# Lo parts of the attention key weights on VectorE, all hi parts on ScalarE, in a one-core hybrid decoder layer

## The chip, the cores and the metric

The kernel runs on one core of a Trainium2 chip. The metric is the device time of one execution in microseconds. Five engines run their own instruction queues, each in order: PE (matmul, with PEld for its weight loads), DVE (VectorE), ACT (ScalarE), POOL (GpSimd) and SP, which here only issues DMAs.

## The reference

One decoder layer over 2048 positions of width 1024: an RMS norm and one input projection feed three mixers, each multiplied by a SiLU gate, and one output projection adds to the residual.

```python
# A) forgetting attention, 8 heads of 64, q and k RMS-normed, c = cumsum(log_sigmoid(f))
sc = q @ k.T * scale + (c[t] - c[s]);  p = softmax(where(s <= t, sc, NEG));  o = p @ v
# B) causal window means over 2/4/8/16 positions minus the token, a 64x64 map per group
# C) stick-breaking attention, 4 heads of 64, strictly causal
log_1m_beta = where(s < t, -softplus(z), 0);  rest = reverse_cumsum(log_1m_beta) - log_1m_beta
a = where(s < t, exp(log_sigmoid(z) + rest), 0);  o = a @ v
out = x + concat(A * silu(g), B * silu(g), C * silu(g)) @ w_out
```

## The kernel before

Rows stand in reverse order in memory, so a query block i (128 rows, 16 blocks) sees keys j*128 to 2048 with j = 15 - i, that is (i+1)*128 of them. All matmuls are float16 pairs: a number is written as a hi part and a lo part (the rest), and three products (hi-hi, hi-lo, lo-hi) are summed in PSUM.

The work falls into four stages that overlap on PE. Phase a is heads 0 to 3 of the forgetting attention, phase b heads 4 to 7, phase s the stick-breaking heads with the pooling mixer among them, and last the output projection. A phase projects q, k, v and gate of block i while the heads of an earlier block run. By the trace below, the attention of a lies at about 58 to 444 us, that of b at 444 to 803, that of s at 803 to 1250, and what is left of the output projection runs to 1416.

A head of a block has one part of keys, or two (96 parts in 64 heads of a phase, of 128 to 1024 columns). What happens to a part in a and b:

- PE makes the scores in one of two PSUM tiles of the pool `sp` (L404), and DVE adds the forget bias, takes the row maximum and writes the tile `L` to SBUF (L736). Only then can PE reuse that PSUM tile.
- ACT takes the exponential in place (L746). `split_t` then writes the hi part as float16 into `pp` (L430 on ACT or L432 on DVE, by the patterns `FHIA` and `FHIB`), and the lo part beside it (L433, a subtraction, on POOL by `FLO`).
- SP issues one DMA transpose of `pp` into `tt` (L435), and PE multiplies `tt` with the values (L446, L447).

In s, ACT takes a sigmoid of the scores into `rr` (L875), POOL masks the first 128 columns of the first part and sets a start column (L877, L878), DVE runs a product scan along the keys (L883), and `split_t` makes hi (ACT, `SHI`) and lo (POOL, `SLO`) of the scan's result, which is transposed and multiplied as before (L903 to L905).

The parts of the softmax or stick weights are what the change calls key weights. `pairs16` (L339) makes the other pairs: hi on ACT, lo on DVE. Of each block it makes those of q and k (tiles `sta`, `stb`, `sts`), of the values and of x (`ppx`); L467 and L469 copy the transposed keys and queries into place on DVE. POOL also has the gain product of k (L718), the division by the softmax sum (L759), the stick rest (L887, L909), the first gate product (L1034) and 16 small DMA issues (L563).

The order of each engine's queue comes from two places: the Python program (a plan that advances the projections against the heads, with lead times by table), and the tile framework's scheduler, which plays the program through a timeline model while it builds it and lets ready instructions pass others. So a change of engine for one instruction can move others.

Of the kernel before, what the change touches and what calls it, by code (L numbers as in the profile page):

```python
# [18 lines left out]
P = 128  # L19
# [44 lines left out]
DEPTH = 3  # L64
TB = 4
PB = 5
FHIA = 'sv'
FHIB = 'ssv'
FLO = 'gg'
SHI = 's'  # L70
SLO = 'gg'
LX = 3
PAT = [5, 7, 9, 10, 11, 12, 12, 12, 13, 14, 14, 14, 15, 15, 15, 15]
XTRA = 29
# [51 lines left out]
def hybrid(ctx: ExitStack, tc, xN, w_in, w_pT, w_out, ng, b_f, qg, kg, w_pool, p_scale, bands, out):  # L126
    nc = tc.nc
    v, s, g, t, sy = nc.vector, nc.scalar, nc.gpsimd, nc.tensor, nc.sync
    S = xN.shape[0]
# [13 lines left out]
    def first(n):  # L143
        return tc.high_priority(offset=n) if n else nullcontext()

    def pick(pattern, k):
        return {"v": v, "g": g, "s": s}[pattern[k % len(pattern)]]
# [240 lines left out]
    def chunks(base):  # L388

        if S - base <= CH:  # L390
            return [(base, S)]
        cut = (base + (512 if base % 512 == 0 else 0)) // 512 * 512 + 512 if not BAL else (S - 512 if base >= S - 1536 else S - CH)
        cut = S - CH if not BAL else cut
        return [(base, cut), (cut, S)]

    def scores(h, qT, Kc, c0, c1_, tag, mask):
        sp = ps.tile([P, 1024], F32, name=f"sp{tag}", tag="sp")
        off = c0 % 512
        b = c0
        while b < c1_:  # L400
            e = min(c1_, (b // 512 + 1) * 512)
            m_ = mask and b == c0
            for a in range(2):
                t.matmul(sp[:, b - c0 + off:e - c0 + off], qT[:, a * NH + h, :], Kc[b // 512][:, h, b % 512:b % 512 + e - b], start=(a == 0), stop=(a == 1 and not m_))  # L404
            if m_:
                t.matmul(sp[:, off:off + P], id16, cmask, start=False, stop=True)
            b = e
        return sp[:, off:off + c1_ - c0]

    def group(n):  # L410

        return 4 if n <= GR4 * P else 2 if n <= GR2 * P else 1
# [3 lines left out]
    def split_t(p32, n, tag, h, all_, hi_eng, lo_eng):  # L416

        G = group(all_)
        k = h % G
        if k == 0:  # L420
            shared["pp"] = at.tile([P, 2 * CH], F16, name=f"pp{tag}", tag="pp", bufs=PB)
            shared["tt"] = at.tile([P, 2 * CH // P, P], F16, name=f"tt{tag}", tag="tt", bufs=TB)
        if G == 1:
            pp, tt = shared.pop("pp"), shared.pop("tt")
        else:
            pp, tt = shared["pp"], shared["tt"]
        o_ = 2 * n * k
        hi, lo = pp[:, o_:o_ + n], pp[:, o_ + n:o_ + 2 * n]
        if hi_eng is s:
            s.copy(hi, p32)  # L430
        else:
            hi_eng.tensor_copy(hi, p32)  # L432
        lo_eng.tensor_tensor(lo, p32, hi, ALU.subtract)  # L433
        if k == G - 1:
            sy.dma_start_transpose(tt[:, :2 * n * G // P, :], pp[:, :2 * n * G])  # L435
        return tt[:, o_ // P:(o_ + 2 * n) // P]
# [57 lines left out]
    class Fox:  # L494
# [227 lines left out]
        def qk(self, i, h):  # L722
            ph, negc = self.ph, self.negc
            j = NT - 1 - i
            qT = self.ctx[i]
            cs = list(chunks(j * P))
            n_ = len(cs)
            mm = sm.tile([P, 2], F32, name=f"mm{ph}_{i}_{h}", tag="mm")
            ls = []
            for a, (c0, c1_) in enumerate(cs):  # L730
                tag = f"{ph}_{i}_{h}_{a}"
                sp = scores(h, qT, self.Kc, c0, c1_, tag, a == 0)
                lt = at.tile([P, CH], F32, name=f"L{tag}", tag="L", bufs=LB)
                lt = lt[:, :c1_ - c0]
                with first(HSP):
                    v.tensor_tensor_reduce(lt, sp, negc[:, h, c0:c1_], c1[:, 0:1], 4 * NEG if a == 0 else mm[:, a - 1:a],  # L736
                                           ALU.add, ALU.max, mm[:, a:a + 1])
                ls.append(lt)
            nm = sm.tile([P, 1], F32, name=f"nm{ph}_{i}_{h}", tag="nm")
            v.tensor_scalar(nm, mm[:, n_ - 1:n_], -1.0, math.log(PS), ALU.mult, ALU.add)  # L740
            if h == 0:
                self.la = sm.tile([P, 2, NH], F32, name=f"la{ph}_{i}", tag="la")
            la = self.la
            parts = []
            for a, (c0, c1_) in enumerate(cs):
                s.activation(ls[a], ls[a], AF.Exp, bias=nm[:, 0:1], accum_out=la[:, a, h:h + 1])  # L746
                tt = split_t(ls[a], c1_ - c0, f"{ph}_{i}_{h}_{a}", h, S - j * P, pick(FHIA if ph == "a" else FHIB, h + a), pick(FLO, h + a))
                parts.append((c0, c1_, tt))
            return parts, (la, n_)

# [36 lines left out]
    class Stick(Fox):  # L787
# [74 lines left out]
        def qk(self, i, h):  # L862
# [6 lines left out]
            for a, (c0, c1_) in enumerate(chunks(j * P)):  # L869
# [14 lines left out]
                rprev = rr[:, n:n + 1]  # L884
                tt = split_t(rr[:, 0:n], n, tag, h, S - j * P, pick(SHI, h + a), pick(SLO, h + a))
                parts.append((c0, c1_, tt))
# [34 lines left out]
    class Pool:  # L921
        ph = "p"
# [91 lines left out]
    class Out:  # L1014
        ph = "o"
# [200 lines left out]
    with tc.manual_schedule(engines={mybir.EngineType.PE}) if MAN else nullcontext():  # L1216
        opening()
        for k, (n, i) in enumerate(plan):
            ph = phases[n]
# [93 lines left out]
```

## Time and profile before

| | us |
|---|---|
| median of 3 runs (1416.5 to 1421.29) | 1419.98 |
| the profiled execution | 1417.73 |
| its span, first to last instruction | 1415.7 |
| PE busy | 1209.6 (85%) |
| DVE busy | 997.1 (70%) |
| ACT busy | 702.0 (50%) |
| POOL busy | 634.1 (45%) |
| mean granted TensorE clock | 0.937 |

The busy shares are means over stages. PE is the busiest engine and is idle for 206 us of the span. An idle PE is read from the waits: which engine or transfer released the instruction that PE stood before.

### The profile page before, as it was taken

What the parts mean: (1) busy time and instruction counts of PE and PEld (TensorE: products, weight loads), DVE (VectorE), ACT (ScalarE), POOL (GpSimd) and SP (SyncE); (2) the same over time, 40 slices, a digit from 0 to 9 for tenths busy, and PEclk for the clock granted to TensorE, in tenths of its full rate; (3) what the DMA queues carried; (4) which work ended last, traced back from release to release, by engine and by line L of the source; (5) the groups of instructions that cost most, each with busy time, mean ns of one, the idle gap of its engine ahead of it and who ended that gap; (6) DMA issues with size and microseconds to landing.
All of it is one profiled execution on the core that took longest, in us unless ns stands there. A gap on an engine that the chain in (4) does not pass through costs nothing.

```text
span 1415.7 us, 24981 instructions
## 1 busy us (share of the span) xinstructions
PE 1209.6 (85%) x9068; PEld 642.2 (45%) x9068; DVE 997.1 (70%) x2093; ACT 702.0 (50%) x1356; POOL 634.1 (45%) x615
## 2 busy tenths in 40 slices
PE   7788879787887889897987888978988997779998
PEld 3344445444444445454544544444544553444443
DVE  5777889889998567786888655556574669865731
ACT  6555546555554446664667644545455564432210
POOL 0133345445455234553656654555455464623300
PEclk9889899999998989999999999999999999989999
DMA  6689999998999999996999998687886888999853
GB/s 215 176 169 203 214 188 221 200 196 182 210 210 209 210 227 207 202 177 135 184 217 191 227 207 186 146 158 161 173 175 142 172 196 226 225 277 287 225 160 89
DMA packets 617068, 275.25 MB, mean 194 GB/s; under 512 B 552561, under 2 KB 590833, under 8 KB 616945
## 3 DMA queue, kind: packets, MB, share of 16 engines
q1 hardware_dynamic: 605600, 239.93, 80.4%
q10 hardware_dynamic: 10832, 33.67, 7.9%
q8 instruction: 71, 1.16, 0.4%
q14 instruction: 53, 0.43, 0.1%
q0 software_dynamic: 512, 0.07, 0.0%
HBM read 102.60 MB, written 34.67 MB: 97 GB/s over the span
## 4 chain that ended last, share of the span: by engine, by line
PE 18%; DVE 11%; issue 9%; DMA 8%; POOL 8%; ACT 5%; SPq 1%; POOLq 0%; ACTq 0%; DVEq 0%
PE pr L319 11%; DVE rrs L883 5%; POOL pps L433 5%; DMA qTs<-sts 2%; DMA qTb<-stb 2%; PE pqks L319 2%; DVE Lb L736 2%; DMA xTm<-ppm 1%; ACT pps L430 1%; ACT Lb L746 1%; POOL rrs L877 1%; PE sps L404 1%; DMA ttb<-ppb 1%; PE pp L319 1%; POOL ppb L433 1%
## 5 line engine op out<-in xcount | busy, mean ns | idle before, releaser
L433 POOL TENSOR_TENSOR ppb<-Lb,ppb 128x1024 f16<-128x1024 f32 (+7 forms) x96 | 151.6, 1593 | 150.3 <-ACT ppb L430 68.9
L433 POOL TENSOR_TENSOR ppa<-La,ppa 128x1024 f16<-128x1024 f32 (+7 forms) x96 | 152.7, 1604 | 141.9 <-DVE ppa L432 53.4
L433 POOL TENSOR_TENSOR pps<-rrs,pps 128x640 f16<-128x640 f32 (+7 forms) x96 | 171.3, 1790 | 75.2 <-ACT pps L430 74.8
L319 PE MATMUL pr<-wo,xTm 128*128 128x512 f16 x768 | 172.2, 386 | 8.1 <-DMA xTm<-ppm 5.3
L883 DVE TENSOR_TENSOR_SCAN rrs<-rrs 128x640 f32<-128x640 f32 (+7 forms) x64 | 109.5, 1714 | 68.3 <-POOL rrs L877 43.8
L430 ACT CAST pps<-rrs 128x640 f16<-128x640 f32 (+7 forms) x96 | 76.1, 796 | 142.0 <-DVE rrs L883 127.3
L746 ACT ACTIVATE Lb<-Lb,nmb 128x640 f32<-128x640 f32 (+7 forms) x96 | 85.6, 892 | 80.3 <-DVE nmb L740 75.4
L746 ACT ACTIVATE La<-La,nma 128x640 f32<-128x640 f32 (+7 forms) x96 | 85.5, 891 | 77.0 <-DVE nma L740 53.5
L319 PEld LDWEIGHTS <-xTm 128*128 128x128 f16 x768 | 75.8, 99 | 100.9 <-issue 8.8
L319 PEld LDWEIGHTS <-xTb 128*128 128x128 f16 x768 | 77.0, 103 | 92.6 <-issue 16.7
L404 PE MATMUL spa<-Ka,qTa 128*128 128x512 f16 (+3 forms) x320 | 83.7, 371 | 36.8 <-DVE mma L736 35.2
L319 PEld LDWEIGHTS <-xTs 128*128 128x128 f16 x768 | 74.4, 99 | 86.9 <-issue 3.3
L319 PEld LDWEIGHTS <-xTx 128*128 128x128 f16 x720 | 72.6, 105 | 89.3 <-issue 25.5
L319 PE MATMUL pqkb<-wb,xTb 128*128 128x512 f16 x384 | 101.7, 408 | 0.3 <-ACT wb L277 0.3
L404 PE MATMUL spb<-Kb,qTb 128*128 128x512 f16 (+3 forms) x320 | 79.7, 361 | 23.4 <-DVE mmb L736 20.7
L319 PE MATMUL pp<-auxp,xTp 128*128 128x512 f16 x384 | 96.9, 404 | 0.0
L319 PE MATMUL pqka<-wa,xTx 128*128 128x512 f16 x336 | 95.3, 434 | 1.3 <-DVE cr L562 1.3
L319 PE MATMUL pvgb<-wb,xTb 128*128 128x512 f16 x384 | 96.1, 390 | 0.0
L875 ACT ACTIVATE rrs<-sps,nc 128x640 f32<-128x640 f32 (+7 forms) x96 | 80.5, 863 | 30.3 <-PE sps L404 28.8
L319 PE MATMUL pqks<-ws,xTs 128*128 128x512 f16 x384 | 92.1, 385 | 0.7 <-DVE vo L342 0.4
L404 PE MATMUL sps<-Ks,qTs 128*128 128x512 f16 (+3 forms) x320 | 73.2, 361 | 21.2 <-DVE qTs L469 16.6
L319 PE MATMUL pvgs<-ws,xTs 128*128 128x512 f16 x384 | 90.9, 379 | 0.0
(307 smaller groups left out, 2804.4 us busy)
## 6 DMA issues: line engine op xcount, KB each, us to landing
xn<-in_xN_dram SPq DMA_DIRECT2D x16, 512.0 KB, 5.5
xTd<-xTx ACTq DMA_DIRECT2D x16, 512.0 KB, 4.3
xTb<-xTd ACTq DMA_DIRECT2D x16, 512.0 KB, 4.6
xTs<-xTd ACTq DMA_DIRECT2D x16, 512.0 KB, 4.3
xTp<-xTd ACTq DMA_DIRECT2D x16, 512.0 KB, 4.3
go<-gat SPq DMA_DIRECT2D x16, 512.0 KB, 7.6
mt<-mix SPq DMA_DIRECT2D x16, 512.0 KB, 5.6
xr<-in_xN_dram SPq DMA_DIRECT2D x16, 512.0 KB, 4.4
```

Source lines behind the costliest of these rows:

```text
L319: t.matmul(psum, x[:, xa, kt, :], wt[:, wa, c0:c0 + n], start=(kt == 0 and i == 0), stop=(kt == KT - 1 and i == 2))
L404: t.matmul(sp[:, b - c0 + off:e - c0 + off], qT[:, a * NH + h, :], Kc[b // 512][:, h, b % 512:b % 512 + e - b], start=(a == 0), stop=(a == ...
L430: s.copy(hi, p32)
L433: lo_eng.tensor_tensor(lo, p32, hi, ALU.subtract)
L736: v.tensor_tensor_reduce(lt, sp, negc[:, h, c0:c1_], c1[:, 0:1], 4 * NEG if a == 0 else mm[:, a - 1:a], ALU.add, ALU.max, mm[:, a:a + 1])
L746: s.activation(ls[a], ls[a], AF.Exp, bias=nm[:, 0:1], accum_out=la[:, a, h:h + 1])
L875: s.activation(gg, sp, AF.Sigmoid, scale=self.nc2[:, 0:1])
L877: g.affine_select(gg[:, 0:P], gg[:, 0:P], [[1, P]], ALU.is_gt, 1.0, base=0, channel_multiplier=-1)
L883: v.tensor_tensor_scan(gg, gg, gg, init, ALU.mult, ALU.bypass)
```

## The change

Two pattern constants become one, and three patterns change. In a and b the hi part of every part goes to ACT (before: every second in a, two of three in b, the rest on DVE). In a, b and s the lo part of every part goes to DVE (before: POOL). One line less at the top moves every later line number up by one: L433 of before is L432 after.

```diff
-FHIA = 'sv'
-FHIB = 'ssv'
-FLO = 'gg'
+FHI = 's'
+FLO = 'v'
 SHI = 's'
-SLO = 'gg'
+SLO = 'v'
...
                 s.activation(ls[a], ls[a], AF.Exp, bias=nm[:, 0:1], accum_out=la[:, a, h:h + 1])
-                tt = split_t(ls[a], c1_ - c0, f"{ph}_{i}_{h}_{a}", h, S - j * P, pick(FHIA if ph == "a" else FHIB, h + a), pick(FLO, h + a))
+                tt = split_t(ls[a], c1_ - c0, f"{ph}_{i}_{h}_{a}", h, S - j * P, pick(FHI, h + a), pick(FLO, h + a))
```

In the first place, DVE's queue where block 8 of phase a runs its heads 1 and 2, the rows before are these (`La_8_2_0` is the tile of block 8, head 2, part 0; `oma` collects results of the block before, `sta` and `qTa` are queries and keys of the next):

```order
L736 ISA La_8_2_0_2740,mma_8_2_2733<-spa_8_2_0_2734,negca_510,c1_170 128x640
L736 ISA mma_8_2_2733 128x1
L342 SCALAR_TENSOR_TENSOR sta_9_2633<-qna_9_2616,sta_9_2633 128x4x64
L740 TENSOR_SCALAR nma_8_1_2682<-mma_8_1_2668 128x1
L780 TENSOR_REDUCE oma_7_2556<-oa_7_2_2715 128x64
L342 SCALAR_TENSOR_TENSOR sta_9_2633<-qna_9_2616,sta_9_2633 128x4x64
L532 SCALAR_TENSOR_TENSOR u10_2808<-pf10_2791,iwa_300,bft_164 128x8
L736 ISA La_8_2_1_2745,mma_8_2_2733<-spa_8_2_1_2742,negca_510,mma_8_2_2733,c1_170 128x512
L736 ISA mma_8_2_2733 128x1
L533 SCALAR_TENSOR_TENSOR u10_2808<-pf10_2791,iwa_300,u10_2808 128x8
L432 CAST ppa_8_1_0_2685<-La_8_1_0_2675 128x640
```

Of the changed kernel, the rows at the same place on DVE are:

```order
L432 TENSOR_TENSOR ppa_8_0_0_2597<-La_8_0_0_2586,ppa_8_0_0_2597 128x640
L432 TENSOR_TENSOR ppa_8_0_1_2603<-La_8_0_1_2591,ppa_8_0_1_2603 128x512
L341 SCALAR_TENSOR_TENSOR sta_9_2633<-qna_9_2616,sta_9_2633 128x4x64
L735 ISA La_8_2_0_2740,mma_8_2_2733<-spa_8_2_0_2734,negca_510,c1_170 128x640
L735 ISA mma_8_2_2733 128x1
L544 TENSOR_SCALAR u10_2808<-u10_2808 128x8
L341 SCALAR_TENSOR_TENSOR sta_9_2633<-qna_9_2616,sta_9_2633 128x4x64
L735 ISA La_8_2_1_2745,mma_8_2_2733<-spa_8_2_1_2742,negca_510,mma_8_2_2733,c1_170 128x512
L735 ISA mma_8_2_2733 128x1
L432 TENSOR_TENSOR ppa_8_1_0_2685<-La_8_1_0_2675,ppa_8_1_0_2685 128x640
L432 TENSOR_TENSOR ppa_8_1_1_2691<-La_8_1_1_2680,ppa_8_1_1_2691 128x512
```

The two lo parts of head 0 now stand ahead of the bias step of head 2 (the step that frees PE's score tile), and those of head 1 behind it; the cast of head 1 is gone to ACT.

In the second place, POOL's queue in block 11 of phase s, the rows before are these (`pps` is the pair, `rrs` the scan's tile, `left` the rest of the stick):

```order
L887 COPY left_11_12797<-rrs_11_0_1_12818 128x1
L433 TENSOR_TENSOR pps_11_0_0_12810<-rrs_11_0_0_12803,pps_11_0_0_12810 128x1024
L433 TENSOR_TENSOR pps_11_0_1_12822<-rrs_11_0_1_12818,pps_11_0_1_12822 128x512
L878 MEMSET rrs_11_2_0_12968 128x1
L877 AFFINE_SELECT rrs_11_1_0_12887<-rrs_11_1_0_12887 128x128
L887 COPY left_11_12797<-rrs_11_1_1_12902 128x1
L433 TENSOR_TENSOR pps_11_1_0_12894<-rrs_11_1_0_12887,pps_11_1_0_12894 128x1024
L433 TENSOR_TENSOR pps_11_1_1_12906<-rrs_11_1_1_12902,pps_11_1_1_12906 128x512
```

and those of the changed kernel, at the same place on POOL:

```order
L886 COPY left_11_12797<-rrs_11_0_1_12818 128x1
L877 MEMSET rrs_11_2_0_12968 128x1
L876 AFFINE_SELECT rrs_11_1_0_12887<-rrs_11_1_0_12887 128x128
L886 COPY left_11_12797<-rrs_11_1_1_12902 128x1
L877 MEMSET rrs_11_3_0_13072 128x1
L876 AFFINE_SELECT rrs_11_2_0_12968<-rrs_11_2_0_12968 128x128
L886 COPY left_11_12797<-rrs_11_2_1_12983 128x1
```

The mask of head 1 stood behind both lo parts of head 0; now no lo part stands between two masks. `left` of head 0 still stands ahead of it.

In the third place, DVE's queue in the same block of phase s of the changed kernel, the lo parts come in behind the scans that make them (L882 is the scan, L880 the copy of its last column into the second part's start):

```order
L882 SCALAR_TENSOR_TENSOR rrs_11_1_0_12887<-rrs_11_1_0_12887 128x1024
L880 COPY rrs_11_1_1_12902<-rrs_11_1_0_12887 128x1
L882 SCALAR_TENSOR_TENSOR rrs_11_1_1_12902<-rrs_11_1_1_12902,rrs_11_1_0_12887 128x512
L432 TENSOR_TENSOR pps_11_1_0_12894<-rrs_11_1_0_12887,pps_11_1_0_12894 128x1024
L466 COPY Ks_12_12840<-qTs_12_12839 128x4x128
L432 TENSOR_TENSOR pps_11_1_1_12906<-rrs_11_1_1_12902,pps_11_1_1_12906 128x512
L468 COPY qTs_12_12839<-qTs_12_12839 64x512 x2
L882 SCALAR_TENSOR_TENSOR rrs_11_2_0_12968<-rrs_11_2_0_12968 128x1024
```

Before, the next head's scan followed with only L467 and L469 between them; now both lo parts stand there too.

On ACT, one sigmoid of the first stick block moves ahead of the last exponentials of phase b, which adds two loads of ACT's function table (six before, eight after, the first at the kernel's start among them).

## Rows read from the trace of the kernel before

**Rows 1.** The page, part 1: busy us (share of the span) and instructions.
```profile
PE 1209.6 (85%) x9068; PEld 642.2 (45%) x9068; DVE 997.1 (70%) x2093; ACT 702.0 (50%) x1356; POOL 634.1 (45%) x615
```
**Rows 2.** Busy us by stage (a, b, s, output), granted clock, DMA share, GB/s.
```profile
core 0: us, PE busy (x) PEld busy (x) DVE busy (x) ACT busy (x) POOL busy (x), PEclk, DMA share, GB/s
57.90:444.00 386.10, 318.21 (x2422) 172.35 (x2422) 330.41 (x876) 213.18 (x479) 180.93 (x141) 0.90 0.97 198
444.00:803.00 359.00, 308.29 (x2321) 169.55 (x2320) 260.80 (x627) 204.80 (x433) 178.12 (x137) 0.95 0.97 197
803.00:1250.00 447.00, 385.65 (x3320) 207.26 (x3320) 287.87 (x343) 224.29 (x349) 243.15 (x310) 0.94 0.84 185
1250.00:1415.70 165.70, 152.05 (x806) 70.34 (x803) 80.69 (x126) 25.30 (x23) 27.84 (x11) 0.96 0.73 203
```
**Rows 3.** Waits over the whole span: who for whom, us, times, longest.
```profile
ACT pps L430 <- DVE rrs L883: 127.3, 78, 5.7
DVE rrs L883 <- POOL rrs L877: 43.8, 28, 4.1
PE spa L404 <- DVE mma L736: 35.2, 20, 4.9
DVE rrs L883 <- POOL rrs L878: 23.8, 9, 3.9
PE spb L404 <- DVE mmb L736: 20.7, 13, 4.1
PE ob L446 <- DMA ttb<-ppb: 20.6, 16, 3.9
PE pd L821 <- ACT vr L341: 18.5, 5, 7.8
PE sps L404 <- DVE qTs L469: 16.6, 5, 7.1
PE oa L446 <- DMA tta<-ppa: 10.7, 6, 3.2
```
**Rows 4.** Groups on POOL, DVE, ACT: busy us, mean ns, idle before and releaser.
```profile
L433 POOL TENSOR_TENSOR pps<-rrs,pps 128x640 f16<-128x640 f32 (+7 forms) x96 | 171.3, 1790 | 75.2 <-ACT pps L430 74.8 <-issue 0.2
L433 POOL TENSOR_TENSOR ppa<-La,ppa 128x1024 f16<-128x1024 f32 (+7 forms) x96 | 152.7, 1604 | 141.9 <-DVE ppa L432 53.4 <-ACT ppa L430 36.3 <-ACT La L746 7.4
L432 DVE CAST ppa<-La 128x1024 f16<-128x1024 f32 (+7 forms) x48 | 28.4, 592 | 12.5 <-ACT La L746 5.2 <-ACT Va L341 3.8 <-DMA tta<-ppa 3.3
L432 DVE CAST ppb<-Lb 128x1024 f16<-128x1024 f32 (+7 forms) x24 | 13.6, 567 | 8.8 <-ACT Lb L746 8.6
L430 ACT CAST ppa<-La 128x1024 f16<-128x1024 f32 (+7 forms) x48 | 37.6, 784 | 4.2 <-DMA xTx<-ppx 3.8
L875 ACT ACT_TABLE_LOAD x3 | 3.8, 1283 | 0.1
L221 DVE TENSOR_TENSOR q_qka<-fa 128x8 f32<-128x8 f32 x16 | 7.4, 465 | 1.7 <-ACT fa L219 1.7
```
**Rows 5.** Single lines on DVE: xcount, ns min/median/max, first and last start.
```profile
L1036 DVE TENSOR_TENSOR mt<-mt,sg x16: 1214/1226/3369, 1185.2 to 1358.5; 128x1024 f32<-128x1024 f32 x16
L221 DVE TENSOR_TENSOR q_qka<-fa x16: 148/158/2012, 42.1 to 381.1; 128x8 f32<-128x8 f32 x16
L469 DVE COPY qTs<-qTs x32: 285/289/2261, 765.0 to 1179.4; 64x512 f16<-64x512 f16 x32
```
**Rows 6.** Timeline at 199 us: start us, us, engine and instruction.
```profile
199.82 4.21 POOL L433 TENSOR_TENSOR ppa<-La,ppa 128x1024 f16<-128x1024 f32 x2 [1.45 <-DVE rla L757]
199.86 2.11 DVE L758 TENSOR_SCALAR rla<-rla,iva 128x4 f32<-128x4 f32 x1
```
**Rows 7.** Timeline at 1116 us, phase s.
```profile
1115.94 2.13 POOL L433 TENSOR_TENSOR pps<-rrs,pps 128x1024 f16<-128x1024 f32 x1
1118.07 0.29 POOL L877 TENSOR_SCALAR_AFFINE_SELECT rrs<-rrs 128x128 f32<-128x128 f32 x1
1118.39 1.76 DVE L883 TENSOR_TENSOR_SCAN rrs<-rrs 128x768 f32<-128x768 f32 x1 [1.27 <-POOL rrs L877]
```

## The prediction

> **What bounds the kernel now.** I read the page's busy shares first [rows 1]: PE is busy for 1209.6 of 1415.7 us, DVE for 997.1, POOL for 634.1. No other engine comes near PE, so time can only be won from PE's 206 us of idleness, or lost by adding to it. The table by stages [rows 2] shows where it lies: 386.1 - 318.2 = 68 us in a, 51 in b, 61 in s, 14 in the output stage. It shows also that DVE is no average engine in a: 330.4 of 386.1 us, 0.86, against 0.73 in b and 0.64 in s.
>
> Third come the waits [rows 3]. In a and b PE stands before score matmuls until DVE has emptied a PSUM tile (35.2 us and 20.7 us), and before value matmuls until a transpose of a weight pair lands (10.7 and 20.6 us). In s, PE waits for an ACT cast of the values (18.5 us in 5 waits) and for DVE's copies of the queries (16.6 us in 5). Behind these stands a ring: ACT's casts wait for DVE's scans (127.3 us), and the scans wait for POOL's mask and start column (43.8 + 23.8 = 67.6 us). The reader can see one turn of it [rows 7]: a lo subtraction holds POOL until 1118.07, the mask of the next head follows it, and the scan starts at 1118.39 after an idle wait of 1.27 us.
>
> Last, I looked at how long equal instructions take. A DVE instruction on 128x8 elements has a median of 158 ns and a maximum of 2012, a copy of 64x512 a median of 289 and a maximum of 2261 [rows 5]. At 199.82 us one sees why [rows 6]: POOL starts a subtraction, DVE starts a 128x4 instruction 0.04 us later, and it takes 2.11 us. It ended at 201.97, just as the first of the two subtractions in that row was over. So a POOL subtraction can stop DVE for its whole length.
>
> The Trainium skill, "SBUF — State Buffer", Who interferes with whom, says the same as a rule: GpSimd's only SBUF port pair is VectorE's second, locked for a whole instruction. The trace agrees by those 2.11 us.
>
> **The change, part by part.**
>
> *The 72 hi casts that leave DVE.* DVE loses 28.4 us in a and 13.6 in b [rows 4]. ACT gains 48 x 784 ns = 38 us in a and 24 x 784 = 19 in b; it then has 251 of 386 and 224 of 359 us. It waits more than it works there, so I cost this at nothing; if the exponentials queued behind the casts, PE would see it as a later transpose.
>
> *The 288 lo subtractions, onto DVE.* Before shows no subtraction of this kind on DVE. The nearest rows are a two-input instruction of 128x1024 at a median of 1226 ns and one of 128x8 at 158 ns [rows 5]: 1.05 ns per column and 0.15 us fixed. A phase has 4 heads x 128 x (1 + ... + 16) = 69,632 columns in 96 parts, so 73.2 + 14.4 = 87.6 us per phase, 0.91 us a part, where POOL took 1.60 to 1.79 [rows 4]. The bounds are the cast's 0.59 us (a lighter instruction) and POOL's own 1.79; I take 0.91, since two inputs are what the 1226 ns row has.
>
> *The stops of DVE, which go.* I took, for each DVE instruction, its time over that of the short ones of its form, where a lo subtraction on POOL lay beside it. A pair of groups shows how: L221 has a mean of 465 ns and a median of 158 [rows 4, 5], over 16 instructions 4.9 us. Summed over all 2093 DVE instructions by this working, that is about 80 us in a, 53 in b and 29 in s. The bounds are none of it (if DVE's time were its own) and all of it.
>
> So DVE's load becomes in a 330.4 - 28.4 + 87.6 - 80 = 310 (0.80 of the stage), in b 260.8 - 13.6 + 87.6 - 53 = 282 (0.79), in s 287.9 + 87.6 - 29 = 347 (0.78). The 175 us that POOL hands over in a and b are nearly paid by the stops that end.
>
> *PE's waits for DVE in a and b.* Before, 35.2 us at a share of 0.86 and 20.7 at 0.73: about 1.1 us for each 0.01 of share. That gives -6 us in a and +6 in b: together 0.
>
> *The transposes.* They are late by what the lo part is late. A part gains 1.66 - 0.91 = 0.75 us, the mean of POOL's three groups taken (the third, of b, is like a's). PE waited in 22 places for `tta` and `ttb` [rows 3], and in s for a few more of `tts`; 28 x 0.75 = 21 us. The subtraction now stands in the longer queue, so I count half: -10 us.
>
> *The ring in s.* No lo part stands between two masks on POOL any more, so most of the 67.6 us go, and with them about half of ACT's 127.3. What ACT holds back behind its casts is the values' cast that PE waits for: half of 18.5 us, -9. The query copies lose the stops (a median of 289 ns against a maximum of 2261): half of 16.6 us, -8. Late next is DVE itself: a head of two parts there has two scans and two subtractions, and the order shows the next scan behind both. At 0.78 that still leaves it idle for 100 us; I give back 1 us of the 17, so -16.
>
> *The new wait.* A subtraction on DVE waits for ACT's hi cast, and what is queued behind it, in a and b, is the bias step that empties PE's score tile. The 72 casts before waited 12.5 + 8.8 = 21.3 us for ACT [rows 4], 0.3 us each. The 192 subtractions of a and b would wait 57 us, 36 more. At 1.1 us of PE wait per 0.01 (3.7 us of DVE's time), that is 36 / 3.7 x 1.1 = 11 us at most. The order puts other rows between (a bias step and query work), so I take 2; the bounds are 0 and 11.
>
> *Two more table loads on ACT*: 2 x 1.28 us [rows 4], between b and s, where ACT holds the first scores of s: +2 us.
>
> Sum: 0 - 10 - 16 + 2 + 2 = -22 us. The profiled execution took 1417.73 us, 2.3 under the median, so 1417.7 - 22 = 1395.7; I forecast 1395.
>
> **The rivals.**
>
> *DVE becomes the bound (slower).* The place is DVE's queue in a and b, the mechanism that a subtraction waiting for ACT's cast holds up the bias steps behind it. For it: DVE's share in a is 0.86 with PE waiting most there, and 0.79 in b is higher than before. Against it: the stops that go are as long, and hit at random, where the new work was in the order from the start. It decides if the stops don't go: then DVE has 330.4 - 28.4 + 87.6 = 390 us in a and 335 in b. With the 12.5 us that it was idle before its casts in a [rows 4], a takes 402 us, +16; in b the share is 0.93, and 20 x 1.1 = 22 us more of waiting. With the 11 us above and the 26 us not won only in part, 1418 + 16 + 22 - 10 = 1446. If half of the stops go, it is about 1428.
>
> *Nothing is won (within 0.3%, which is about what a measurement of this kernel can tell from no change).* PE's queue is in order and its order is planned; a wait that goes in one place can come back at the next product that depends on the same plan. For it: after the ring comes the output stage, which needs all of s; the DMA share is 0.97 in a and b [rows 2], so transposes that are issued earlier may land as late. Then 1418.
>
> The Trainium skill, "Perfetto Trace Analysis", Optimizing Scalar/DVE Operations, speaks against the change with a rule of this result: as the two engines share a read port, moving work between them might not help. By that rule the port is held as long as before. The rows say otherwise for this move, 0.91 us against 1.66 a part, so it has the chance of this case and no more.
>
> *Much more is won.* If the stops were what made nearly all of PE's waits in a and b (35.2 + 20.7 + 10.7 + 20.6 = 87 us) and half of these go, with the 16 of s: 1418 - 60 = 1358. For it: the stops fall on short instructions of a chain (norms of q and k) that no plan allows for. Against it: the subtractions put as much time into the same queue.
>
> That the change doesn't do what it says I exclude: the order shows 288 lo parts on DVE and none on POOL.
>
> **How the numbers follow.** The forecast, between 1370 and 1410, has 0.40; much more won (below 1370) 0.17; nothing won, 0.10; the remainder is slower, 0.33, which is the DVE rival between 1424 and 1450. Faster by over 0.3% is below 1415.7: the first two with a little of 1410 to 1415, 0.58; the same 0.09; slower above 1424, 0.33. The range from 1355 to 1446 leaves out the ends of both sides, about 0.1 each; the forecast's own range is 1370 to 1410.
>
> **What would show it.** DVE's busy time near 310, 282 and 347 us in the stages, and 128x8 rows with no maximum of 2 us, show the stops gone; subtractions with a mean near 0.91 us show the price. The waits of scans for POOL should fall from 67.6 us to under 20, and PE's waits for `ttb` and `tta` together to about 20. Wrong would be: DVE rows of L432 with long idle waits for ACT's L429, and PE waiting more than 56 us for DVE's bias steps; or, without either, PE's waits moved to products of s or to transposes that land no earlier.

## The result and the profile after

The changed kernel took 1405.53 us in the median of 4 runs (1397.48 to 1408.75) against 1419.67: a ratio of 0.9899, 95% interval 0.9863 to 0.9934. A second series beside other kernels gave 1404.51 us and 0.9927 (0.9903 to 0.9950). So it is faster by about 1%, 12 to 14 us, where the forecast's sum had 22. One execution of one experiment (e3, 1437.36 us) lay more than 1.5% above the fastest of its kernel and is left out of its ratio and median.

The profiled execution took 1408.75 us, its span 1407.0. The busy line of its page, which answers to [rows 1]:

```profile
PE 1199.0 (85%) x9068; PEld 637.2 (45%) x9068; DVE 1036.6 (74%) x2309; ACT 752.8 (54%) x1430; POOL 182.1 (13%) x327
```

POOL is down by 452 us, DVE up by 40. PE is idle for 1407.0 - 1199.0 = 208 us, which is no less than before (206); what is shorter is PE's busy time, for the same 9068 matmuls. The granted clock's mean was 0.937 in the profile before and 0.941 in this one; over more executions that difference does not hold, as the part on why the prediction was right shows.

The stages, in the columns of [rows 2] and cut at the same times (so not at quite the same instructions):

```profile
57.90:444.00 386.10, 307.31 (x2390) 166.90 (x2390) 302.95 (x913) 238.13 (x518) 32.36 (x47) 0.92 0.97 199
444.00:803.00 359.00, 310.72 (x2341) 170.91 (x2342) 275.56 (x700) 222.27 (x459) 29.23 (x40) 0.93 0.94 193
803.00:1250.00 447.00, 389.65 (x3380) 209.94 (x3377) 347.36 (x459) 233.02 (x358) 93.08 (x215) 0.94 0.85 191
```

DVE's 303, 276 and 347 us stand beside a forecast of 310, 282 and 347. The groups show why: a subtraction takes 0.92 to 0.94 us, and the short instructions are no longer stopped for long (columns as in [rows 4], then [rows 5]).

```profile
L432 DVE TENSOR_TENSOR ppb<-Lb,ppb 128x640 f16<-128x640 f32 (+7 forms) x96 | 88.9, 936 | 11.3 <-ACT ppb L429 10.8
L432 DVE TENSOR_TENSOR ppa<-La,ppa 128x640 f16<-128x640 f32 (+7 forms) x96 | 88.2, 934 | 7.0 <-ACT ppa L429 6.7 <-issue 0.2
L432 DVE TENSOR_TENSOR pps<-rrs,pps 128x640 f16<-128x640 f32 (+7 forms) x96 | 87.3, 919 | 17.0 <-ACT pps L429 15.6 <-DMA tts<-pps 0.7
L220 DVE TENSOR_TENSOR q_qka<-fa 128x8 f32<-128x8 f32 x16 | 2.5, 155 | 0.1
```
```profile
L220 DVE TENSOR_TENSOR q_qka<-fa x16: 138/156/168, 41.5 to 379.5; 128x8 f32<-128x8 f32 x16
L468 DVE COPY qTs<-qTs x32: 286/289/343, 764.8 to 1177.8; 64x512 f16<-64x512 f16 x32
```

This 128x8 group fell from a maximum of 2012 ns to 168, the copies of the queries of s from 2261 to 343. The waits, which answer to [rows 3]:

```profile
ACT pps L429 <- DVE rrs L882: 113.8, 78, 7.3
PE oa L445 <- DMA tta<-ppa: 35.0, 22, 7.5
PE ob L445 <- DMA ttb<-ppb: 31.5, 18, 4.2
DVE rrs L882 <- POOL rrs L876: 18.9, 25, 3.2
PE pd L820 <- ACT vr L340: 17.5, 7, 4.6
PE spa L403 <- DVE mma L735: 16.0, 14, 4.2
PE sps L403 <- DVE qTs L468: 13.5, 5, 5.2
DVE rrs L882 <- POOL rrs L877: 7.5, 5, 5.2
PE spb L403 <- DVE mmb L735: 5.0, 5, 2.5
```

Two groups of PE's waits have changed places. Before score matmuls PE waits 16.0 + 5.0 = 21 us (before 55.9), before value matmuls 35.0 + 31.5 = 66.5 us (before 31.3): 35 us won and 35 us lost. In s the scans wait 18.9 + 7.5 = 26.4 us for POOL, where it was 67.6. The prediction had named a sign of being wrong that has come: PE's waits moved to the transposes, 66.5 us where it had expected about 20. Of its other signs, the scans' waits stayed over the 20 us that it gave, and the 2 us rows went as it said. A turn of the ring in s, to set beside [rows 7]:

```profile
1109.50 1.90 ACT L874 ACTIVATE rrs<-sps,nc 128x768 f32<-128x768 f32 x2
1110.47 0.30 POOL L876 TENSOR_SCALAR_AFFINE_SELECT rrs<-rrs 128x128 f32<-128x128 f32 x1 [2.04 <-ACT rrs L874]
1110.80 1.76 DVE L882 TENSOR_TENSOR_SCAN rrs<-rrs 128x768 f32<-128x768 f32 x1 [0.32 <-POOL rrs L876]
```

POOL now waits for ACT's sigmoid (2.04 us) and masks at once, with no lo part in front; the scan waits for the mask for 0.32 us, where it was 1.27. DVE's own lo part, which stands before this scan, had ended only those 0.32 us earlier.

### The profile page after: what moved, and what is told of

The parts are those of the page before. It is cut to its first block, busy times and chain, and to the rows that moved or that the text cites. A ratio compares the mean times of both kernels' runs of the same rounds, so it can differ in the third digit from the quotient of the medians.

```text
span 1407.0 us, 24844 instructions
## 1 busy us (share of the span) xinstructions
PE 1199.0 (85%) x9068; PEld 637.2 (45%) x9068; DVE 1036.6 (74%) x2309; ACT 752.8 (54%) x1430; POOL 182.1 (13%) x327
## 4 chain that ended last, share of the span: by engine, by line
PE 40%; DMA 25%; DVE 15%; issue 9%; ACT 8%; POOL 2%; SPq 1%; ACTq 0%; DVEq 0%; POOLq 0%
PE pr L318 10%; DMA tta<-ppa 6%; DVE rrs L882 5%; DMA ttb<-ppb 5%; PE pqkb L318 4%; PE pvgb L318 4%; DMA xTx<-ppx 3%; PE pqks L318 3%; DMA qTa<-sta 3%; PE pp L318 2%; PE spb L403 2%; PE pqka L318 2%; PE pvgs L318 2%; DMA xTm<-ppm 2%; PE ob L445 2%
## 5 line engine op out<-in xcount | busy, mean ns | idle before, releaser
L882 DVE TENSOR_TENSOR_SCAN rrs<-rrs 128x640 f32<-128x640 f32 (+7 forms) x64 | 106.4, 1663 | 27.2 <-POOL rrs L876 18.9
L745 ACT ACTIVATE Lb<-Lb,nmb 128x640 f32<-128x640 f32 (+7 forms) x96 | 85.5, 892 | 62.4 <-DVE nmb L739 59.4
L745 ACT ACTIVATE La<-La,nma 128x640 f32<-128x640 f32 (+7 forms) x96 | 85.4, 890 | 48.7 <-DVE nma L739 42.5
L318 PEld LDWEIGHTS <-xTx 128*128 128x128 f16 x720 | 69.8, 101 | 83.2 <-issue 13.9
L432 DVE TENSOR_TENSOR pps<-rrs,pps 128x640 f16<-128x640 f32 (+7 forms) x96 | 87.3, 919 | 17.0 <-ACT pps L429 15.6
L318 PE MATMUL pqkb<-wb,xTb 128*128 128x512 f16 x384 | 97.0, 399 | 1.6 <-DVE oma L779 1.3
L432 DVE TENSOR_TENSOR ppb<-Lb,ppb 128x640 f16<-128x640 f32 (+7 forms) x96 | 88.9, 936 | 11.3 <-ACT ppb L429 10.8
L318 PE MATMUL pqks<-ws,xTs 128*128 128x512 f16 x384 | 95.6, 394 | 0.2 <-DVE vo L341 0.2
L403 PE MATMUL spa<-Ka,qTa 128*128 128x512 f16 (+3 forms) x320 | 79.6, 363 | 18.5 <-DVE mma L735 16.0
L432 DVE TENSOR_TENSOR ppa<-La,ppa 128x640 f16<-128x640 f32 (+7 forms) x96 | 88.2, 934 | 7.0 <-ACT ppa L429 6.7
L445 PE MATMUL oa<-Va,tta 128*128 128x128 f16 x544 | 61.9, 227 | 36.3 <-DMA tta<-ppa 35.0
L445 PE MATMUL ob<-Vb,ttb 128*128 128x128 f16 x544 | 63.3, 226 | 32.7 <-DMA ttb<-ppb 31.5
L318 PE MATMUL pqka<-wa,xTx 128*128 128x512 f16 x336 | 87.7, 407 | 1.5 <-DVE nma L739 1.5
```

The costliest lines, as they stand in the source:

```text
L318: t.matmul(psum, x[:, xa, kt, :], wt[:, wa, c0:c0 + n], start=(kt == 0 and i == 0), stop=(kt == KT - 1 and i == 2))
L445: t.matmul(o[:, 0:P], tt[:, b, :], vt, start=first, stop=False)
L882: v.tensor_tensor_scan(gg, gg, gg, init, ALU.mult, ALU.bypass)
```

## The experiments

Theory A came from the waits above: the gain is the ring in s, while in a and b the change wins nothing. Theory B put the gain into a and b. As the change has three switches (hi casts of a and b on ACT, lo parts of a and b on DVE, lo parts of s on DVE), the first experiments set them one by one. Each edit also lets the scheduler reorder all queues, so a difference of two kernels holds the effect of that order too. Ratios are to the kernel before, measured beside each experiment; the experiments ran in three such series, and two that are of different series are compared by their ratios.

**Only s (e1).** The kernel before, with

```diff
-SLO = 'gg'
+SLO = 'v'
```

> Only the stick-breaking phase has its lo parts on VectorE; phases a and b as before. Theory A (the gain is the ring in s: masks behind lo parts): nearly all of the changed kernel's 14 us, so a ratio of 0.990 to 0.993, and the scans' waits for GpSimd fall from 67.6 us to about 26. Theory B (the gain is in a and b, where PE's waits for score tiles fell from 56 to 21 us): a ratio of 0.998 to 1.002 in spite of the shorter waits of the scans.

Measured: 1407.57 us, ratio 0.9932 (0.9905 to 0.9959); the scans waited 26.6 + 7.7 = 34 us for POOL, where A had 26. B falls, and the time is A's to within 0.0002 of its range: s alone is worth 10 us.

**Only a and b (e2).** The changed kernel, with

```diff
-SLO = 'v'
+SLO = 'gg'
```

> Hi casts on ScalarE and lo parts on VectorE in phases a and b alone; phase s as before. Theory A: 0.997 to 1.003, since what PE wins on score tiles (about 35 us) comes back as waits for transposes (about 31 us). Theory B: 0.988 to 0.993, as the whole change.

Measured: 1425.71 us, 1.0067 (1.0042 to 1.0091): slower. PE waited 16.0 + 4.8 us for score tiles and 28.0 + 34.1 for transposes, the exchange that the whole change shows. That this costs more than it wins was in neither theory. (The profile is of the fastest of the six executions, 1417.31 us.)

**Lo parts on DVE, hi casts as before (e3).** The kernel before, with `FLO = 'v'` and `SLO = 'v'`.

> All lo parts on VectorE, but the hi casts by the patterns of before (72 of 192 in a and b on VectorE). Theory A': the longer wait for transposes in a comes from ScalarE, which now makes all casts (from an exponential's end to the hi part's end it took 3.1 us in a, 2.0 before); then this kernel has fewer of PE's 35 us of waits for tta and is 0.5 to 1% faster than the whole change, ratio 0.980 to 0.985. Theory B' (VectorE's load decides): 42 us more on VectorE, ratio 0.992 to 1.000.

Measured: 1426.16 us, 1.0049 (1.0018 to 1.0080); the executions lie in two groups, five from 1412 to 1420 us, the profiled one among them, and six from 1426 to 1433. A' falls: leaving casts on DVE makes it slower, not faster, than the whole change. B' was nearer, though it lies even above B's range of 0.992 to 1.000. Against e1, of the same series and different in these alone, the lo parts of a and b on DVE cost 1.0049 / 0.9932, 1.2%.

**Five buffers for transposed pairs (e6).** The changed kernel, with

```diff
-TB = 4
-PB = 5
+TB = 5
+PB = 4
```

> The changed kernel with five instead of four buffers for transposed pairs (tt), and four instead of five for the pairs (pp), for space. Theory C (transposes start late because they wait for a free tt buffer, which PE gives back: SP waited for PE's value products 106 us in the changed kernel, 38 before): PE's waits for tta, ttb and tts fall from 73 us to under 50, ratio 0.975 to 0.985. Rival (they are late because the lo part stands late in VectorE's queue, or by the missing pp buffer): ratio 0.990 to 1.000 and the same waits.

Measured: 1405.0 us, 0.9918 (0.9892 to 0.9943), the changed kernel's time. PE's waits for `tta`, `ttb` and `tts` were 24.1 + 29.3 + 4.5 = 58 us, where the changed kernel had 74 and theory C under 50, and the time saved there did not show. SP's own waits before a transpose for PE's products of `oa`, `ob` and `os` add up to 56.0 + 32.9 + 15.9 = 105 us, where the changed kernel has 47.9 + 37.5 + 20.3 = 106: the fifth buffer did not shorten the wait that theory C put down to it. So the time speaks for the rival, but the run does not show what the kernel would do without that wait. Whether the lost `pp` buffer took a gain away was not tried.

**The change again (e10).** No edit.

> The changed kernel once more, unedited, beside the three others. All theories: a ratio of 0.987 to 0.993 as before; a second profile shows how far one stage of the same program differs from run to run (the same instructions of phase a took 387 us from first to last in the changed kernel and 378 us in the kernel with phase s undone).

Measured: 1404.51 us, 0.9927 (0.9903 to 0.9950). PE waited 31.4 + 34.9 us for transposes and 15.5 + 4.7 for score tiles, so the exchange is no accident of one profile. From PE's first score matmul of a to its first of b it took 382.4 us, where the first profile had 387.3: one stage of one program differs by some us between executions, so smaller differences of a stage are not read here.

**Hi casts on ACT, lo parts on DVE in s alone (e9).** The changed kernel, with

```diff
-FLO = 'v'
+FLO = 'gg'
```

> Hi casts all on ScalarE and the lo parts of s on VectorE; the lo parts of a and b stay on GpSimd. Theory A (in a and b the lo parts on VectorE are no gain, what helps there is that VectorE loses 72 casts): as fast as the whole change or faster, ratio 0.985 to 0.991. Theory D (the stops of VectorE by GpSimd's subtractions cost time in a and b, and the whole change wins there by their end): ratio 0.993 to 0.998, with 130 to 150 us of VectorE instructions prolonged in a and b.

Measured: 1378.38 us, 0.9739 (0.9712 to 0.9766). It beats both kernels, the changed one of the same series by 26 us, and lies below the ranges of both theories. Its busy line and waits:

```profile
PE 1195.5 (86%) x9068; PEld 636.1 (46%) x9068; DVE 994.3 (72%) x2117; ACT 750.6 (54%) x1428; POOL 480.8 (35%) x519
```
```profile
PE spa L403 <- DVE mma L735: 26.7, 18, 6.7
DVE rrs L882 <- POOL rrs L876: 20.1, 26, 3.3
PE spb L403 <- DVE mmb L735: 17.6, 17, 2.6
PE ob L445 <- DMA ttb<-ppb: 16.9, 13, 5.7
PE oa L445 <- DMA tta<-ppa: 14.5, 9, 3.8
```

PE waits 44 us for score tiles and 31 for transposes, 76 in place of the change's 88, and is idle for 187 us in all. Theory D, that the whole change wins in a and b by the end of DVE's stops, falls: by the prediction's working on this trace 113 us of stops are still there in a and b (theory D had 130 to 150), and it is faster.

**Junk subtractions on POOL (e5).** The changed kernel, with `LX = 2` and, in `split_t`, a subtraction on POOL that nobody waits for (`junk` is a tile of its own, made once):

```diff
+    junk = const.tile([P, CH], F16, name="junk")
...
         lo_eng.tensor_tensor(lo, p32, hi, ALU.subtract)
+        wide = [P, n // P, P]
+        g.tensor_tensor(junk[:, 0:n].rearrange("p (a b) -> p a b", b=P), ones.unsqueeze(1).broadcast_to(wide), ident.unsqueeze(1).broadcast_to(wide), ALU.subtract)
```

> The changed kernel, and beside each lo part on VectorE a subtraction of the same length on GpSimd whose result nobody uses (it reads two constants in SBUF); two instead of three row buffers for space. Theory D (GpSimd's subtractions stop VectorE): VectorE's busy time rises by 100 us or more over the changed kernel's 1037 us, 128x8 instructions have maxima near 2 us again, and the time is 3 to 6% over the changed kernel, 1450 to 1490 us. Rival (VectorE's long rows had another cause, or are free): within 1% of the kernel with memsets in their place.

Measured: 1619.83 us, 1.1441 (1.1411 to 1.1471). DVE's busy time is 1345.2 us, 309 over the changed kernel's, for the same instructions:

```profile
PE 1266.1 (78%) x9068; PEld 662.6 (41%) x9068; DVE 1345.2 (83%) x2309; ACT 756.6 (47%) x1430; POOL 728.1 (45%) x615
```
```profile
L221 DVE TENSOR_TENSOR q_qka<-fa x16: 138/158/2309, 58.4 to 507.3; 128x8 f32<-128x8 f32 x16
L471 DVE COPY qTa<-qTa x32: 286/290/2407, 80.4 to 547.7; 64x512 f16<-64x512 f16 x32
```

The stops are back, and with the next experiment beside it, which has the same buffers, POOL's subtractions cause them. The junk, 548 us of it, ran without waiting for anything and was over at 866 us. The time is far over the 3 to 6% expected, and it went where the junk ran: PE's first score matmul of a came at 81.5 us for 53.5, from there to the first of b it took 504 us for 387, from there to the first of s 415 for 358, and s itself, behind the junk, took 9 us more. It was not POOL's queue: the waits of others for POOL's products of k were 2.5 + 1.6 us.

**Memsets on POOL (e7).** The same, with `g.memset(junk[:, 0:n], 1.0)` for the subtraction.

> The same as the junk subtractions, but with GpSimd writing as many columns by memset, which reads nothing; the same two row buffers. Theory D with the narrower reading (only what GpSimd reads stops VectorE's two-input instructions): VectorE's rows stay near those of the changed kernel save for copies and casts, and the time lies within 1% of it, 1400 to 1420 us. Wider reading (whatever GpSimd does stops VectorE): as slow as the junk subtractions in proportion to GpSimd's busy time.

Measured: 1422.86 us, 1.0057 (1.0032 to 1.0083), with 203 us of memsets, all in the first 303 us. The two-input instructions are hardly touched, the copies for up to a memset's length:

```profile
L221 DVE TENSOR_TENSOR q_qka<-fa x16: 144/159/303, 42.2 to 387.1; 128x8 f32<-128x8 f32 x16
L470 DVE COPY qTa<-qTa x32: 286/290/1022, 53.8 to 416.4; 64x512 f16<-64x512 f16 x32
```

The narrower reading fits the rows in the main. Counted over the trace, of the two-input rows (TENSOR_TENSOR) with nothing but a memset beside them on POOL, 6 of 129 took over 0.15 us longer than the short ones of their group; beside a junk subtraction in e5 it was 80 of 138. Of copies it was 16 of 36, where e5 had 36 of 47. The six are the part that it leaves unexplained: a 128x1 row took 814 ns for 159 and ended as a memset did. The time is 1.3% over the changed kernel of the same series, where 1% was the bound; the two row buffers for three were not tried alone.

**Only the hi casts (e4).** The kernel before, with `FHI = 's'` for `FHIA` and `FHIB`.

> Only the hi casts of a and b move to ScalarE; every lo part stays on GpSimd. Theory E (the parts add: the casts are worth about 27 us, phase s about 10): ratio 0.978 to 0.984. Rival (the casts help only where GpSimd's queue is also free of the lo parts of s, or the gain was made by the order): ratio 0.990 to 1.000.

Measured: 1394.14 us, 0.9821 (0.9798 to 0.9844). Theory E holds: 25 us by the casts alone, and the rival falls. With e1 the product is 0.9821 x 0.9932 = 0.9754, and e9, which has both, measured 0.9739: without lo parts of a and b on DVE the two parts add. So theory A, too, came near by a cancellation: in a and b the casts win what the lo parts lose. Against e4, e2's lo parts of a and b on DVE cost 1.0067 / 0.9821, 2.5%.

```profile
57.90:444.00 386.10, 319.39 (x2495) 175.03 (x2493) 302.18 (x855) 248.75 (x545) 188.69 (x148) 0.91 1.00 206
444.00:803.00 359.00, 314.83 (x2404) 173.88 (x2405) 251.21 (x601) 227.06 (x464) 184.31 (x164) 0.97 0.99 204
```

In these stretches of e4 DVE has 28 and 10 us less than before, and PE passes 2495 and 2404 matmuls where it passed 2422 and 2321. PE's waits for score tiles are 26.5 + 17.3 = 44 us, where they were 56.

**Value products one head later (e11).** The changed kernel, with

```diff
-DEPTH = 3
+DEPTH = 4
```

> The changed kernel with value products issued one head later in the program (DEPTH 4 for 3), so that in b 264 rows stand on PE between a head's scores and its value products, where the changed kernel has 213 and the one before 248. Theory F (the lo parts on VectorE lose time in a and b because the scheduler, which counts on earlier lo parts, moves the value products ahead, and PE then waits for transposes): PE's waits for tta and ttb fall from 67 us to 40 or less, and the time by 10 us or more, ratio 0.975 to 0.985. Rival (VectorE's queue itself costs the time): the waits move to score tiles, ratio 0.988 to 1.000.

Measured: 1408.46 us, 0.9908 (0.9882 to 0.9935): no gain, so theory F falls as it was set down. The waits did as it says, but others took their place:

```profile
PE spa L403 <- DVE mma L735: 24.3, 13, 6.9
PE ob L445 <- DMA ttb<-ppb: 23.6, 13, 8.0
PE oa L445 <- DMA tta<-ppa: 13.7, 9, 6.8
PE spb L403 <- DVE mmb L735: 4.4, 8, 1.4
```

The transposes went from 66.5 to 37.3 us, the score tiles from 21 to 28.7; PE's waits for query copies grew (13.5 to 20.3 us in s), and it was idle for 215 us (span 1414.0, PE busy 1198.6). The test is no clean one: a greater depth holds each pair longer, and ACT's casts of s now stand before a transpose that has yet to read the old pair. In the changed kernel, then here:

```profile
ACT pps L429 <- DMA tts<-pps: 13.4, 6, 4.4
```
```profile
ACT pps L429 <- DMA tts<-pps: 78.0, 38, 11.9
```

**The same for the fastest kernel (e13).** e9 with `DEPTH = 4`.

> Hi casts on ScalarE, lo parts of s on VectorE, those of a and b on GpSimd, and DEPTH 4. Theory F holds that the slack counts where the value products stood too near: here the distance in b was that of before (248), so little is to be won, ratio 0.968 to 0.980. Rival (a greater depth helps any of these kernels alike): by as much as it helps the changed kernel.

Measured: 1413.4 us, 0.9954 (0.9933 to 0.9975), 2.2% slower than e9, which neither side had expected. The greater depth costs by itself, and here too ACT's casts of s wait for transposes, 81.7 us where e9 has 12.0. At that depth the lo parts of a and b are no loss on DVE: e11 is 0.9908 to e13's 0.9954. So their price is not a fixed one; whether the order around them or the new wait hides it was not told apart.

**Every second lo part of a and b on DVE (e15).** e9 with `FLO = 'gv'`.

> As the kernel with hi casts on ScalarE and the lo parts of s on VectorE, but every second lo part of a and b on VectorE, the others on GpSimd. If the loss by lo parts on VectorE grows with their number: halfway between 0.974 and 0.991, so 0.980 to 0.986. If the order on PE decides it (241 rows between scores and value products in b, near the 248 of the faster kernel): 0.972 to 0.978.

Measured: 1390.54 us, 0.9787 (0.9756 to 0.9817): 0.5% over e9, where the whole move costs 1.9%. It lies between the two ranges that were set down, and does not tell them apart.

## Why the prediction was right, and which steps were not

The direction was right, the range held the time, and the forecast of 1395 was 10 us too low. But the sum that gives it is not what happened: two of its terms are wrong by 25 us and more, with opposite signs. Step by step:

- *DVE's load.* Right: 303, 276 and 347 us for 310, 282 and 347. The subtraction's 0.91 us was measured as 0.93, and the stops of about 162 us went: in the changed kernel no lo part is left on POOL to cause one. e5 shows their cause.
- *The ring in s.* Right in its mechanism (67.6 us of scans' waits became 26.4), forecast at 16 us, worth 10 by e1 and 12 by e9 against e4, but 20 to 24 where the lo parts of a and b are on DVE too (the whole change, 0.9927 and 0.9899, against e2's 1.0067). The waits that were to fall by half, PE's for the values' cast (18.5 to 17.5) and for the query copies (16.6 to 13.5), hardly fell. What PE won in s stands in no single wait.
- *The hi casts.* This step was the first that failed. "I cost this at nothing" looked at ACT, where the casts go, and not at DVE, where they leave: the 42 us were entered in DVE's load and then priced with the rest, at nothing. e4 shows 25 us.
- *PE's waits for DVE in a and b, and the transposes.* Forecast 0 and -10 us; measured -35 and +35. The step that failed is that the lo part comes 0.75 us earlier because it takes 0.75 us less. It comes later. The traces give these means over the 96 parts of a and of b, in us from end to end (the last row to the first product's start):

| a / b | before | e9 | changed | changed, e10 |
|---|---|---|---|---|
| bias step to exponential | 3.8 / 3.1 | 3.5 / 3.2 | 4.3 / 4.1 | 4.3 / 4.1 |
| exponential to hi part | 2.0 / 1.8 | 2.5 / 2.0 | 3.1 / 1.8 | 3.1 / 1.8 |
| hi part to lo part | 2.3 / 2.1 | 2.4 / 2.2 | 2.6 / 2.3 | 2.5 / 2.3 |
| lo part to first product | 13.3 / 10.5 | 12.8 / 10.1 | 12.2 / 8.3 | 12.1 / 8.3 |

  From the bias step to the lo part's end it is 10.1 us in a and 8.2 in b, where e9, which differs in the lo parts of a and b alone, has 8.4 and 7.4. What a subtraction saves on DVE it loses by waiting in DVE's queue (hi to lo), and most of the delay lies in front of it. Between a head's last bias step and L739, the small DVE instruction that gives the exponential its shift, the changed kernel has 33 lo subtractions in the 64 heads of a and 42 in b; in e9 they are on POOL, and L739 ends 0.5 us sooner in a and 0.35 in b. At the same time the value products stand closer to the lo parts in b. So PE stood before them more often.
- *The new wait.* Smaller than forecast: the subtractions of a and b found DVE idle for 18.3 us, 10.8 + 6.7 of it for ACT, where the step had 57 on DVE and took 2 of them for PE. The step looked at the subtraction's wait for ACT and not at what its own length holds up.
- *The table loads.* The two more are there, 1.28 us each; what they cost was not tried.

In sum, the casts are worth about -25 us, the ring -10 to -12, and the lo parts of a and b on DVE +17 to +35 by the three comparisons (1.2, 1.9 and 2.5%), where the prediction had them at -8 with the new wait and all. The three do not simply add: beside lo parts of a and b on DVE the ring is worth 20 to 24 us and the casts 17 to 21 (the whole change against e3). That the forecast came near is luck: the casts that it priced at nothing and the loss that it took for a gain nearly cancel. The rival "DVE becomes the bound" named the place and the sign for a and b, and a queue that holds up what stands behind a subtraction; but it meant the bias steps and a subtraction that waits for ACT, and PE's wait for the bias steps fell.

The traces also show where the time went. From PE's first score matmul of a stage to its first of the next, and in s to its last value product, in us:

| | a | b | s |
|---|---|---|---|
| before | 386.5 | 355.2 | 484.5 |
| e4, casts alone | 373.3 | 344.8 | 484.5 |
| e9, casts and s | 376.2 | 348.3 | 471.3 |
| changed | 387.3 | 358.2 | 475.2 |
| changed, e10 | 382.4 | 358.8 | 479.2 |

The casts win 13 us in a and 10 in b, the ring wins in s, and the lo parts of a and b lose 10 us in b again and 6 to 11 in a. Against e9 the changed kernel's PE is idle for 21 us longer: 35 more for transposes, 23 less for score tiles, and 9 elsewhere.

A wait turns into time in a second way. Between the profiles of before and of the changed kernel PE's idleness rose by 2 us and the time fell by 8.7, all of it in PE's busy time. The rows of the granted clock have two levels, 1.2 and 2.4 GHz. The span had 178 us at the lower one before, 167 after and 148 in e9, and in them PE was busy for 146, 125 and 118 us. From one 128x512 projection matmul to the next it is 216 ns at the upper level and 427 at the lower, so about half of the busy time at the lower one is lost. By that the changed kernel should win 10.6 us and e9 13.9; PE's busy time fell by 10.6 and 14.1. But this differs from execution to execution. In e10, the changed kernel again, PE was busy for 141 us at the lower level and for 1203.7 in all. Over the ten executions beside it the clock's mean was 0.937, against 0.941 for the kernel before: the change did not raise it. In e9 and e4 it was 0.947, against 0.941 and 0.940, and all six executions of e4 lay above all twelve of before.

What stays open is how 192 later parts come to 17 to 35 us. The exchange of waits, the later parts and the lo subtractions in front of the exponentials are shown; that the last are the reason was not tried, for instance by an order that keeps L739 ahead of them. Against it stands that ACT's own wait for L739 did not grow (42.5 + 59.4 us, in e9 43.0 + 80.2). e6 and e11 left the time as it was, but neither took its supposed cause away cleanly. The lo parts of a and b on DVE with the casts and s as before, the one combination of the three switches that is missing, was not run.

## What to carry to other kernels

A change with three switches is three changes: set each alone before believing the sum, since here one was worth -25 us, one -10 and one +17 to +35, and the best kernel (0.9739) has two of them. Moving work off an engine that PE waits for can be worth more than its busy share tells. Moving other work onto it can give that back even where its busy time stays the same: in a, DVE was busy for 301 us in e9's stretch and for 303 in the changed kernel's, and the stage took 6 to 11 us longer. A quicker step in a longer queue is not an earlier one: look at when its result is ready, and at what now stands behind it, not only at its duration. And ask of a right forecast whether its terms were right.

## What the runs showed of the hardware

- A POOL subtraction with its inputs in SBUF can stop DVE instructions of two SBUF inputs, and copies, for up to its own run: 128x8 rows of 158 ns took up to 2.0 us before and 2.3 in e5, where 548 us of such POOL work added 309 us to DVE. POOL memsets (e7) left the 128x8 rows shown at 0.30 us or less and copies at 1.02 us or less. The Trainium skill, "SBUF — State Buffer", Who interferes with whom, says that a two-input VectorE instruction contends with a GpSimd instruction that reads SBUF, not with one that only writes. These rows agree in the main, 80 of 138 two-input rows beside subtractions and 6 of 129 beside memsets; the six do not.
- PE's busy time for the same matmuls differs from profile to profile by what it does at the lower level of its clock: 1209.6 us before, 1199.0 and 1203.7 in two profiles of the changed kernel, 1195.5 in e9, with 146, 125, 141 and 118 us busy at 1.2 GHz. The mean of the granted clock does not tell it (0.937, 0.941, 0.933 and 0.947): in e10 it was lower than before, and PE was busy for 5.9 us less.
